# Block scales of an MLP: a max over 128 partitions through DRAM instead of through TensorE, an earlier weight load and seven PSUM banks

## The chip, the cores and the metric

The kernel runs on one core of a Trainium2 chip. The metric is the device time in microseconds (us) of one execution; lower is better. Engines are named as the profile names them: PE is the matrix engine (TensorE), PEld its weight load, DVE is VectorE, ACT is ScalarE, POOL is GpSimd, and SP is the engine that issues the DMAs. PE accumulates in PSUM, which has banks of 128 x 512 float32.

## The reference

One layer of an encoder with 512 tokens and width 1024. The first half (two attention branches, gates and an output projection) is not touched by the change. The second half is

```python
x = x + mixed                       # mixed ends in a product with w_out
h = rms_norm(x, norm_ffn[l])
x = x + jnp.square(jax.nn.relu(h @ w_up[l])) @ w_down[l]   # w_up 1024x4096, w_down 4096x1024
```

## The kernel before

**Products with halves.** The MLP needs more precision than one float16 product gives. Each operand is scaled by a power of two and split into a high and a low float16 half, and each product is three matmuls: high by high, high by low, low by high (`three`, lines 140 to 142). For a block of weights, `split` makes the high half on ACT (line 114) and the low half on DVE (line 115).

**Blocks.** The MLP is a list of 16 blocks (`order`): "u" blocks are 1024 x 512 pieces of w_up, "d" blocks pieces of w_down. In order they are u u u d d u u d d u u u d d d d, numbered 0 to 15. A block has four chunks of 128 x 1024 float32 (512 KB each); PE goes through chunk 0 for four output tiles, then chunk 1, and so on: 16 steps of 6 matmuls, 96 matmuls of 512 columns. Block 0 is done in two halves of 256 columns. Blocks alternate between two sets of SBUF places, so the load of a chunk of block n+2 waits until PE has left the same chunk of block n.

**A block's scale.** `Block.stage(c)` loads a chunk and takes its absolute maximum per partition on DVE (line 818). `Scale.gather` takes the maximum of the four (line 775), lets PE transpose that column into a row (line 777) and takes the row's maximum (line 779). `Scale.spread` lets PE copy the result to all partitions by a product with a column of 2^-14 (line 784), and DVE makes the scale and its inverse (lines 786, 787). Only then can the four `split`s of the block run. There are 20 such scales: one for each block, and one for each quarter q of the hidden activations (`rows[q]`), whose maxima come from ACT's `accum_out` as ACT writes the squared results of the last u block of a quarter (lines 943, 946). The split activations (`split_a`) are the other operand of the d blocks.

**Order.** A scheduler sets each engine's order from the program's order and buffers; instructions under `pin` keep the program's order on their engine. `tick` counts PE's steps; `later(k, f)` runs f at k steps from now, and `prepare` yields once a step. Engines run their instructions strictly in their order. A block's results wait in four PSUM banks (pool `pg`) until ACT or DVE has taken them; three more banks (pool `pm`) serve transposes and scales.

**The transition.** `gemm_rows` (line 199) does the last projection (w_out) in four row tiles. Behind each, x is added (line 856), normalised (`renorm`, line 246), transposed by PE and split. Beside it `staged(blocks[0])` prepares block 0. Block 1's places are still taken by w_out, so it is loaded after `gemm_rows`.

Of the kernel before, what the change touches and what calls it, by code (L numbers as in the profile page):

```python
# [19 lines left out]
P = 128  # L20
# [17 lines left out]
def hybrid_layer(ctx: ExitStack, tc: tile.TileContext, x, norm_mix, w_in, a_q_norm, a_k_norm,  # L38
# [47 lines left out]
    def tick():  # L86
        clock[0] += 1
        due = [w for w in waiting if w[0] <= clock[0]]
        for w in due:
            waiting.remove(w)  # L90
        for w in sorted(due, key=lambda w: w[:2]):
            w[2]()

    def bank(name):
        return pm.tile([P, 512], F32, tag="m", name=name, bufs=3)
# [660 lines left out]

    bound = const.tile([P, 8, 13], F32, name="bound")
    nc.gpsimd.memset(bound, 2.0 ** -60)
    col14 = const.tile([1, P], F32, name="col14")
    nc.gpsimd.memset(col14, 2.0 ** -14)  # L760
    slots = [0]

    class Scale:


        def __init__(self, n):
            self.n = n
            self.m = bound[:, slots[0] % 8, :]
            slots[0] += 1
            self.both = bound[:, (slots[0] - 1) % 8, 9:13]  # L770
            self.by, self.inv = self.both[:, 0:1], self.both[:, 1:2]

        def gather(self):
            top = self.both[:, 2:3]
            nc.vector.tensor_reduce(top, self.m[:, 0:self.n + 1], axis=AX.X, op=ALU.max)
            self.ps = bank("scale")
            pin(nc.tensor.transpose(self.ps[0:1, 0:P], top, ident))
            one = self.both[0:1, 3:4]
            nc.vector.tensor_reduce(one, self.ps[0:1, 0:P], axis=AX.X, op=ALU.max)
            nc.vector.tensor_scalar(one.bitcast(I32), one.bitcast(I32), 0x7F800000, None,  # L780
                                    op0=ALU.bitwise_and)

        def spread(self):
            pin(nc.tensor.matmul(self.ps[:, 256:257], col14, self.both[0:1, 3:4], start=True,  # L784
                                 stop=True))
            nc.vector.tensor_copy(self.inv, self.ps[:, 256:257])
            nc.vector.reciprocal(self.by, self.inv)

    gs = const.tile([P, 4], F32, name="gs")
# [13 lines left out]
    class Block:  # L803
# [4 lines left out]
            self.tags = places[n % 2]  # L808
            self.raw, self.hilo = [], []

        def stage(self, c):
            if c == 0:
                self.scale = Scale(4)
            t = act.tile([P, 4 * 512], F32, tag=self.tags[c], name="w16")
            raw = t[:, 0:1024]
            parts = t[:, 1024:2048].bitcast(F16).rearrange("p (n k c) -> p n k c", n=2, k=KC)
            nc.sync.dma_start(raw.rearrange("p (k c) -> p k c", k=KC), self.src[c])
            nc.vector.tensor_reduce(self.scale.m[:, c:c + 1], raw, axis=AX.X, op=ALU.max,  # L818
                                    apply_absolute_value=True)
            self.raw.append(raw.rearrange("p (k c) -> p k c", k=KC))  # L820
            self.hilo.append((parts[:, 0], parts[:, 1]))

        def split(self, c):
            split(*self.hilo[c], self.raw[c], scale=self.scale.by)

    order = [("u", 0, 0), ("u", 0, 1), ("u", 1, 0), ("d", 0, 0), ("d", 0, 1), ("u", 1, 1),
             ("u", 2, 0), ("d", 1, 0), ("d", 1, 1), ("u", 2, 1), ("u", 3, 0), ("u", 3, 1),
# [2 lines left out]
              Block(w_down_v[:, q * KD:(q + 1) * KD, :], g * 512, n)  # L830
              for n, (kind, q, g) in enumerate(order)]

    def prepare(b):

        b.scale.gather()
        yield
        yield
        b.scale.spread()
        yield
        for c in range(4):  # L840
            b.split(c)
            yield
            yield

    def staged(b):
        for c in range(4):
            b.stage(c)
            yield
            yield
        yield from prepare(b)  # L850

    def add_to_x2(cb, then=None, scale=None):
        def f(i, ps):
# [20 lines left out]
        xn = normed(x2[:, i, :], gbf)  # L874
        later(6, lambda: transposed(xn, i, hh, hl))

    side = staged(blocks[0])
    gemm_rows(chunks, mh, ml, add_to_x2(1, renorm), side=side)
    for _ in side:
        pass  # L880
# [1 line left out]

    raws, rows, parts16 = {}, {}, {}
    for c in range(4):
        blocks[1].stage(c)

    def products(n, tokens_out, ah, al, evac, halves=False, finish=None):
        b = blocks[n]
        pss = [pg.tile([P, 512], F32, tag="g", name="g") for _ in range(4)]
        extra = bank("extra") if finish is not None else None  # L890
        ready = prepare(blocks[n + 1]) if n + 1 < len(blocks) else iter(())
        nxt = blocks[n + 2] if n + 2 < len(blocks) else None
        step = [0]

        def tick16():
            step[0] += 1
            if step[0] >= 4:
                next(ready, None)
            tick()

        if halves:
            for half in range(2):
                cols = slice(half * 256, half * 256 + 256)
                for i in range(4):
                    for c in range(4):
                        part(pss[i][:, cols], False, i, c * KC, KD, b.hilo[c], ah, al, cols)
                        if c % 2:
                            tick16()
                    if half == 1:
                        evac(i, pss[i])  # L910
            if nxt is not None:
                for c in range(4):
                    nxt.stage(c)
        else:
            for c in range(4):
                for i in range(4):
                    if finish is not None and i == 3:
                        for half, ps in enumerate((pss[3], extra)):
                            cs = slice(half * 256, half * 256 + 256)
                            part(ps[:, 0:256], True, i, c * KC, KD,  # L920
                                 [w[:, :, cs] for w in b.hilo[c]], ah, al)
                            if c == 3:
                                finish(ps[:, 0:256], cs)
                        continue
                    part(pss[i], tokens_out, i, c * KC, KD, b.hilo[c], ah, al)
                    if c == 3:
                        evac(i, pss[i])
                    tick16()
                if nxt is not None:
                    nxt.stage(c)  # L930
        for _ in ready:
            pass

    def up(n, q, g):
        if g == 0:
            raws[q] = act.tile([P, KD, S], F32, tag=("mh", "ml")[q % 2], name="a")
            rows[q] = Scale(8)
        inv = sm.tile([P, 1], F32, tag="inv", name="inv")
        nc.vector.tensor_tensor(inv, blocks[n].scale.inv, inv_h, op=ALU.mult)

        def evac(i, ps):
            r = sc.tile([P, 512], F32, tag="sA", name="relu")
            nc.scalar.activation(r, ps, AF.Relu, scale=inv)
            k = 4 * g + i

            nc.scalar.activation(raws[q][:, k, :], r, AF.Square,
                                 accum_out=rows[q].m[:, k:k + 1])
            if k == KD - 1:
                later(4, rows[q].gather)
                later(6, rows[q].spread)  # L950
                for k0 in range(0, KD, KC):
                    later(7 + k0, lambda k0=k0: split_a(q, k0))

        products(n, False, hh, hl, evac, halves=n == 0)

# [56 lines left out]
```

## Time and profile before

| what | value |
|---|---|
| time, median of 3 runs (lowest, highest) | 741.26 us (740.2, 742.75) |
| the profiled execution: its own time, its span | 741.79 us, 740.1 us |
| PE busy | 724.6 us, 98% of the span |
| DVE busy, ACT busy | 429.5 us, 299.8 us |
| block 0 starts; blocks 1 to 15 start; last matmul starts | 382.8; 408.15; 736.37 us |
| granted PE clock | full (2.4 GHz), but half from 419.03 to 422.44 us |

The span is the time from the first to the last instruction; the 1.7 us between it and the execution's own time lie around it. PE's busy time counts overlapping matmuls, so that the time from one matmul's start to the next says more than "busy".

### The profile page before, as it was taken

Reading aid. Unit: us, or ns where it says so; the run is one execution under the profiler, and the core shown is the slowest. Engines: PE = TensorE matmul, PEld = TensorE weight load, DVE = VectorE, ACT = ScalarE, POOL = GpSimd, SP = SyncE. Lnnn points to the kernel's source line nnn. Section 1 sums busy time; section 2 is a strip of 40 time slices with the busy share of each in tenths; the row PEclk is TensorE's granted clock in tenths of the full one; section 3 lists DMA queues with packets and bytes.
Section 4 is the critical chain, followed back from the end, with each engine's and each line's share of the span. In section 5 each row is a group of like instructions: output and inputs, shape, how many; then the busy total and the mean of one; then the engine's idle time right before and its main releaser. Section 6 shows DMA issues by size and latency. Waiting matters only on the chain.

```text
span 740.1 us, 8777 instructions
## 1 busy us (share of the span) xinstructions
PE 724.6 (98%) x3514; PEld 470.6 (64%) x3514; DVE 429.5 (58%) x656; ACT 299.8 (41%) x464; POOL 58.4 (8%) x73
## 2 busy tenths in 40 slices
PE   7999999999999999999999899999999999999998
PEld 4777778888777888888878444444444444444444
DVE  5557475746566545448286637665656658557541
ACT  6444445435455842333054345223650157361020
POOL 4300215000000002103010000000000000000000
PEclk9999999999999999999999999999999999999999
DMA  6703312122211632433030533323233332322211
GB/s 231 242 22 89 111 58 85 58 86 67 76 58 61 201 109 86 134 120 117 0 115 2 160 96 98 101 89 111 86 101 99 101 100 85 107 93 85 86 58 57
DMA packets 37899, 71.03 MB, mean 96 GB/s; under 512 B 3745, under 2 KB 5089, under 8 KB 37858
## 3 DMA queue, kind: packets, MB, share of 16 engines
q1 hardware_dynamic: 37858, 70.47, 30.5%
q8 instruction: 27, 0.44, 0.2%
q14 instruction: 14, 0.11, 0.0%
HBM read 68.36 MB, written 2.10 MB: 95 GB/s over the span
## 4 chain that ended last, share of the span: by engine, by line
PE 83%; DMA 7%; DVE 6%; ACT 1%; POOL 1%; issue 1%; SPq 0%; DVEq 0%; POOLq 0%
PE g L140 25%; PE g L142 25%; PE g L141 24%; DMA w<-in_w_down_dram 4%; DVE bound L818 2%; DMA w<-in_w_up_dram 2%; PE poa L663 2%; DVE w L115 1%; DMA wst<-in_w_in_dram 1%; DVE xn L246 1%; PE scale L784 1%; PE ps L591 1%; PE ps L587 1%; PE ptp L75 1%; PE pa L499 1%
## 5 line engine op out<-in xcount | busy, mean ns | idle before, releaser
L114 ACT ACTIVATE w<-w,bound 128x1024 f16<-128x1024 f32 x64 | 68.5, 1138 | 141.6 <-PE scale L784 49.8
L818 DVE TENSOR_REDUCE bound<-w 128x1 f32<-128x1024 f32 x64 | 77.7, 1217 | 68.4 <-DMA w<-in_w_down_dram 35.9
L142 PE MATMUL g<-h,w 128*128 128x512 f16 (+1 forms) x288 | 102.9, 358 | 0.7 <-DVE w L115 0.7
L141 PE MATMUL g<-h,w 128*128 128x512 f16 (+1 forms) x288 | 102.7, 357 | 0.3 <-DVE h L112 0.3
L140 PE MATMUL g<-h,w 128*128 128x512 f16 (+1 forms) x288 | 102.6, 358 | 0.0
L140 PE MATMUL g<-w,a 128*128 128x512 f16 (+1 forms) x256 | 96.2, 376 | 0.7 <-DVE x L858 0.7
L142 PE MATMUL g<-w,a 128*128 128x512 f16 (+1 forms) x256 | 96.2, 376 | 0.0
L141 PE MATMUL g<-w,a 128*128 128x512 f16 (+1 forms) x256 | 96.2, 376 | 0.0
L112 DVE TENSOR_TENSOR wl<-wst,wh 128x1024 fp32r<-128x1024 f32 x48 | 59.6, 1244 | 59.5 <-ACT wh L111 59.3
L115 DVE SCALAR_TENSOR_TENSOR w<-w,bound 128x1024 f16<-128x1024 f32 x64 | 78.8, 1279 | 2.7 <-ACT w L114 2.6
L111 ACT CAST wh<-wst 128x1024 fp32r<-128x1024 f32 x48 | 50.3, 1050 | 70.2 <-PE g L141 47.2
L140 PE MATMUL g<-uh,wh 128*128 128x512 f32 x160 | 64.9, 406 | 0.0
L142 PE MATMUL g<-uh,wl 128*128 128x512 f32 x160 | 62.6, 391 | 0.0
L141 PE MATMUL g<-ul,wh 128*128 128x512 f32 x160 | 62.5, 391 | 0.0
L140 PE MATMUL g<-wh,uh 128*128 128x512 f32 x128 | 52.9, 413 | 0.3 <-DVE qt L458 0.3
L141 PE MATMUL g<-wl,uh 128*128 128x512 f32 x128 | 50.1, 392 | 0.0
L142 PE MATMUL g<-wh,ul 128*128 128x512 f32 x128 | 50.0, 392 | 0.0
L142 PEld LDWEIGHTS <-w 128*128 128x128 f16 x288 | 28.3, 98 | 29.2 <-issue 1.4
L140 PEld LDWEIGHTS <-w 128*128 128x128 f16 x288 | 28.3, 98 | 25.8 <-issue 0.8
L142 PEld LDWEIGHTS <-a 128*128 128x128 f16 x264 | 25.8, 98 | 29.5
L141 PEld LDWEIGHTS <-w 128*128 128x128 f16 x288 | 28.3, 98 | 25.3 <-issue 0.8
L141 PEld LDWEIGHTS <-a 128*128 128x128 f16 x264 | 25.8, 98 | 28.7 <-issue 1.0
(239 smaller groups left out, 1128.0 us busy)
## 6 DMA issues: line engine op xcount, KB each, us to landing
wst<-in_w_in_dram SPq DMA_DIRECT2D x41, 512.0 KB, 3.7
w<-in_w_up_dram SPq DMA_DIRECT2D x32, 512.0 KB, 3.7
w<-in_w_down_dram SPq DMA_DIRECT2D x32, 512.0 KB, 3.8
wst<-in_w_branch_dram SPq DMA_DIRECT2D x8, 512.0 KB, 3.8
wst<-in_w_out_dram SPq DMA_DIRECT2D x8, 512.0 KB, 4.0
xs<-in_x_dram SPq DMA_DIRECT2D x4, 512.0 KB, 7.0
x<-in_x_dram SPq DMA_DIRECT2D x4, 512.0 KB, 7.2
out_dram<-x SPq DMA_DIRECT2D x7, 256.0 KB, 2.0
```

Source lines behind the costliest of these rows:

```text
L75: ins = nc.tensor.transpose(out[:, i, :], block, ident)
L111: first(nc.scalar.copy(hi, src))
L112: first((engine or nc.vector).tensor_tensor(lo, src, value(hi), op=ALU.subtract))
L114: nc.scalar.activation(hi, src, AF.Identity, scale=scale)
L115: nc.vector.scalar_tensor_tensor(lo, src, scale, value(hi), op0=ALU.mult, op1=ALU.subtract)
L140: nc.tensor.matmul(ps, ah, bh, start=start, stop=False)
L141: nc.tensor.matmul(ps, ah, bl, start=False, stop=False)
L142: nc.tensor.matmul(ps, al, bh, start=False, stop=stop)
L246: first(nc.vector.scalar_tensor_tensor(xn[j], src[:, cs], r, g, op0=ALU.mult, op1=ALU.mult))
L499: nc.tensor.matmul(pa[:, hs, :], kd[:, c, t * P:(t + 1) * P], qz[:, c, t], start=True, stop=True)
L663: nc.tensor.matmul(po[:, h, :], pT[0][:, k, :], av[:, k, h * P:(h + 1) * P], start=(k == 0), stop=(k == t))
L818: nc.vector.tensor_reduce(self.scale.m[:, c:c + 1], raw, axis=AX.X, op=ALU.max, apply_absolute_value=True)
```

## The change

Four parts. (1) `Scale.gather` no longer uses PE: the column of maxima is written to DRAM by a DMA from POOL's queue and read back by a second one as a row on every partition; `spread` takes the maximum of that 128 x 128 tile on DVE. (2) Loads and maxima are separate (`load`, `top`); the maximum of a chunk is put 3 steps behind its load. In `prepare` the gather comes at step 6 instead of 4, the spread at step 12 instead of 6, and the four splits at steps 12, 13, 14 and 15 instead of 7, 9, 11 and 13. For `rows` the gather comes 2 steps after the last result instead of 4 and the spread 8 instead of 6. (3) Block 1 is loaded during `gemm_rows`, into a place of its own (`ul`). (4) Results rotate through seven banks: four of `pg`, three of `pm`.

```diff
         def gather(self):
             top = self.both[:, 2:3]
-            nc.vector.tensor_reduce(top, self.m[:, 0:self.n + 1], axis=AX.X, op=ALU.max)
-            self.ps = bank("scale")
-            pin(nc.tensor.transpose(self.ps[0:1, 0:P], top, ident))
-            one = self.both[0:1, 3:4]
-            nc.vector.tensor_reduce(one, self.ps[0:1, 0:P], axis=AX.X, op=ALU.max)
+            pin(nc.vector.tensor_reduce(top, self.m[:, 0:self.n + 1], axis=AX.X, op=ALU.max))
+            there = tc.dram_tile([1, P], F32, name="tops")
+            nc.gpsimd.dma_start(there.rearrange("o p -> p o"), top)
+            self.row = wp.tile([P, P], F32, tag="st", name="row", bufs=4)
+            nc.gpsimd.dma_start(self.row, there.broadcast_to([P, P]))
+
+        def spread(self):
+            one = self.both[:, 3:4]
+            pin(nc.vector.tensor_reduce(one, self.row, axis=AX.X, op=ALU.max))
             nc.vector.tensor_scalar(one.bitcast(I32), one.bitcast(I32), 0x7F800000, None,
                                     op0=ALU.bitwise_and)
-
-        def spread(self):
-            pin(nc.tensor.matmul(self.ps[:, 256:257], col14, self.both[0:1, 3:4], start=True,
-                                 stop=True))
-            nc.vector.tensor_copy(self.inv, self.ps[:, 256:257])
+            nc.vector.tensor_scalar(self.inv, one, 2.0 ** -14, None, op0=ALU.mult)
             nc.vector.reciprocal(self.by, self.inv)
...
+        def top(self, c):
+            pin(nc.vector.tensor_reduce(self.scale.m[:, c:c + 1], self.raw[c], axis=AX.X,
+                                        op=ALU.max, apply_absolute_value=True))
...
-    def prepare(b):
-
+    def prepare(b, wait):
+
+        for _ in range(wait):
+            yield
         b.scale.gather()
-        yield
-        yield
+        for _ in range(6):
+            yield
         b.scale.spread()
-        yield
         for c in range(4):
             b.split(c)
             yield
+
+    def first_blocks():
+        for c in range(4):
+            blocks[0].load(c)
+        raw = act.tile([P, 4, 1024], F32, tag="ul", name="raw1")
+        for c in range(4):
+            blocks[1].load(c, raw[:, c, :])
+        yield
+        yield
+        for c in range(4):
             yield
...
+            blocks[0].top(c)
+        yield from prepare(blocks[0], 1)
...
-    side = staged(blocks[0])
+    side = first_blocks()
...
     for c in range(4):
-        blocks[1].stage(c)
+        blocks[1].place(c)
+        blocks[1].top(c)
+    turn = [0]
+
+    def psum():
+        turn[0] += 1
+        if turn[0] % 7 < 4:
+            return pg.tile([P, 512], F32, tag="g", name="g")
+        return bank("g")
...
-        pss = [pg.tile([P, 512], F32, tag="g", name="g") for _ in range(4)]
...
-        ready = prepare(blocks[n + 1]) if n + 1 < len(blocks) else iter(())
+        pss = [psum() for _ in range(4)]
...
+        ready = prepare(blocks[n + 1], 5) if n + 1 < len(blocks) else iter(())
...
+        def load_next(c):
+            if nxt is not None:
+                nxt.load(c)
+                later(3, lambda: nxt.top(c))
...
-                later(4, rows[q].gather)
-                later(6, rows[q].spread)
+                later(2, rows[q].gather)
+                later(8, rows[q].spread)
                 for k0 in range(0, KD, KC):
-                    later(7 + k0, lambda k0=k0: split_a(q, k0))
+                    later(8 + k0, lambda k0=k0: split_a(q, k0))
```

**ACT at the end of block 5**, a u block that ends a quarter. The four `w` tiles are the high halves of block 6; relu (line 943 before, 964 after) and square (946, 967) take block 5's results; `a` tiles are the activations' high halves, done in block 6. Before:

```order
L114 ACTIVATE w_3813<-w_3813,bound 128x1024
L114 ACTIVATE w_3845<-w_3845,bound 128x1024
L114 ACTIVATE w_3876<-w_3876,bound 128x1024
L114 ACTIVATE w_3909<-w_3909,bound 128x1024
L943 ACTIVATE relu<-g,inv 128x512
L946 ACTIVATE a,bound<-relu 128x512
```

and in the changed kernel:

```order
L114 ACTIVATE w_3815<-w_3815,bound 128x1024
L114 ACTIVATE w_3847<-w_3847,bound 128x1024
L964 ACTIVATE relu<-g,inv 128x512
L114 ACTIVATE w_3880<-w_3880,bound 128x1024
L967 ACTIVATE a,bound<-relu 128x512
L964 ACTIVATE relu<-g,inv 128x512 x2
L967 ACTIVATE a,bound<-relu 128x512 x2
L114 ACTIVATE w_3917<-w_3917,bound 128x1024
L964 ACTIVATE relu<-g,inv 128x512
L967 ACTIVATE a,bound<-relu 128x512
L114 ACTIVATE a_4128<-a,bound 128x1024 x4
```

The high halves of the next block now stand between the results; the last square, which completes the maxima of `rows`, stands behind all four.

**DVE in block 6**, behind the low halves of block 6. `bound` holds the maxima and scales, `w_3979` and up (before) or `w_4015` and up (after) are chunks of blocks 7 and 8, `a` the activations' low halves, and `w_3947` or `w_3950` is chunk 0 of block 7. Before:

```order
L786 COPY bound<-scale 128x1
L787 RECIPROCAL bound<-bound 128x1
L786 COPY bound<-scale 128x1
L115 SCALAR_TENSOR_TENSOR a_4116<-a,bound,a_4116 128x1024
L818 TENSOR_REDUCE bound<-w_4095 128x1
L787 RECIPROCAL bound<-bound 128x1
L115 SCALAR_TENSOR_TENSOR a_4116<-a,bound,a_4116 128x1024 x2
L115 SCALAR_TENSOR_TENSOR w_3947<-w_3947,bound 128x1024
```

and in the changed kernel, from the spread of `rows` on (line 781 reads the row that came back from DRAM; the second one is block 7's):

```order
L781 TENSOR_REDUCE bound<-row 128x1
L782 TENSOR_SCALAR bound<-bound 128x1
L784 TENSOR_SCALAR bound<-bound 128x1
L785 RECIPROCAL bound<-bound 128x1
L115 SCALAR_TENSOR_TENSOR a_4128<-a,bound,a_4128 128x1024
L826 TENSOR_REDUCE bound<-w_4099 128x1
L115 SCALAR_TENSOR_TENSOR a_4128<-a,bound,a_4128 128x1024
L826 TENSOR_REDUCE bound<-w_4138 128x1
L115 SCALAR_TENSOR_TENSOR a_4128<-a,bound,a_4128 128x1024
L781 TENSOR_REDUCE bound<-row 128x1
L115 SCALAR_TENSOR_TENSOR a_4128<-a,bound,a_4128 128x1024
L782 TENSOR_SCALAR bound<-bound 128x1
```

Behind the last of these rows come two more small instructions, line 985, and then the low half of `w_3950`. Block 7's scale, which before stood among the first of the activations' low halves, now stands behind all four of them and two maxima.

**POOL in blocks 5, 6 and 7.** Before, POOL has no instruction there. Now it has these; `tops_4076` is the column of `rows`, `tops_4114` that of block 7:

```order
L775 DMA tops_3965<-bound_2715 128x1
L777 DMA row_3967<-tops_3965 128x128
L775 DMA tops_4076<-bound_2715 128x1
L775 DMA tops_4114<-bound_2715 128x1
L777 DMA row_4078<-tops_4076 128x128
L777 DMA row_4116<-tops_4114 128x128
```

Where a quarter's scale and a block's scale fall into one block (blocks 2, 6, 10 and 12), the reading back of the first stands behind the writing of the second.

## Rows read from the trace of the kernel before

**Rows 1.** Page: span, and busy time of each engine, share, instructions.

```profile
span 740.1 us, 8777 instructions
...
PE 724.6 (98%) x3514; PEld 470.6 (64%) x3514; DVE 429.5 (58%) x656; ACT 299.8 (41%) x464; POOL 58.4 (8%) x73
```

**Rows 2.** Stretches: length, busy us of each engine, granted clock, DMA share, GB/s.

```profile
408.15:736.50 328.35, 324.08 (x1520) 147.72 (x1517) 191.37 (x264) 114.88 (x159) 0.00 (x0) 0.99 0.30 94
...
419.03:422.44 3.41, 3.41 (x10) 1.17 (x9) 3.38 (x5) 3.37 (x4) 0.00 (x0) 0.50 0.00 0
```

**Rows 3.** Timeline of PE, end of block 0 and end: start, duration, instruction.

```profile
408.04 0.27 PE L142 MATMUL g<-h,w 128*128 128x256 f16 x1
408.15 0.38 PE L140 MATMUL g<-h,w 128*128 128x512 f16 x1
408.37 0.38 PE L141 MATMUL g<-h,w 128*128 128x512 f16 x1
...
736.37 0.27 PE L142 MATMUL extra<-w,a 128*128 128x256 f16 x1
```

**Rows 4.** Timeline of PE in block 1, around the scale of block 2.

```profile
415.06 0.38 PE L142 MATMUL g<-h,w 128*128 128x512 f16 x1
417.42 0.27 PE L777 MATMUL scale<-ident,bound 128*1 128x128 f32 x1 [1.98 <-DVE bound L775]
...
420.28 0.63 PE L142 MATMUL g<-h,w 128*128 128x512 f16 x1
420.70 0.63 PE L140 MATMUL g<-h,w 128*128 128x512 f16 x1
```

**Rows 5.** Timeline of PE, start of block 13.

```profile
673.07 0.38 PE L142 MATMUL g<-w,a 128*128 128x512 f16 x1
674.16 0.38 PE L140 MATMUL g<-w,a 128*128 128x512 f16 x1 [0.71 <-DVE x L858]
```

**Rows 6.** Groups by line, blocks 1 to 15: busy us, mean ns, idle before.

```profile
L115 DVE SCALAR_TENSOR_TENSOR w<-w,bound 128x1024 f16<-128x1024 f32 x56 | 68.8, 1279 | 1.6 <-ACT w L114 1.5
L818 DVE TENSOR_REDUCE bound<-w 128x1 f32<-128x1024 f32 x56 | 68.2, 1218 | 66.1 <-DMA w<-in_w_down_dram 35.9 <-DMA w<-in_w_up_dram 29.7
...
L858 DVE SCALAR_TENSOR_TENSOR x<-g,inv,x 128x512 f32<-128x512 f32 x31 | 22.6, 747 | 29.9 <-PE g L142 29.9
...
L784 PE MATMUL scale<-bound,col 1*128 1x1 f32 x36 | 6.8, 256 | 0.0
...
L777 PE MATMUL scale<-ident,bound 128*1 128x128 f32 x18 | 4.9, 271 | 3.6 <-DVE bound L775 3.1
```

**Rows 7.** Timelines of DVE and PE in the transition.

```profile
367.07 1.42 DVE L246 SCALAR_TENSOR_TENSOR xn<-x,rx,gb_ffn 128x512 f32<-128x512 f32 x2 [2.14 <-POOL rx L101]
369.69 0.69 DVE L856 TENSOR_TENSOR x<-x,g 128x512 f32<-128x512 f32 x1 [1.20 <-PE g L142]
...
388.45 3.47 DVE L818 TENSOR_REDUCE bound<-w 128x1 f32<-128x1024 f32 x3
...
382.82 0.28 PE L140 MATMUL g<-h,w 128*128 128x256 f16 x1
```

**Rows 8.** DMA from issue to landing: chunk loads (line 817), small columns (327), small rows (354).

```profile
DMA to landing us min/median/max: 3.5/3.8/7.3
...
DMA to landing us min/median/max: 2.0/2.3/3.9
...
DMA to landing us min/median/max: 2.9/3.3/3.9
```

**Rows 9.** Timeline of ACT at the start of block 6, and the load that starts with it.

```profile
519.71 3.88 DMA w<-in_w_down_dram
...
520.54 0.63 ACT L946 ACTIVATE a<-relu 128x512 f32<-128x512 f32 x1
521.08 0.19 ACT L946 ACTIVATION_READ_ACCUMULATOR a<-relu 128x1 f32 x1
527.44 4.26 ACT L114 ACTIVATE a<-a,bound 128x1024 f16<-128x1024 f32 x4 [6.18 <-DVE bound L787]
531.62 4.25 ACT L114 ACTIVATE w<-w,bound 128x1024 f16<-128x1024 f32 x4
```

More of the change, by code (lines that the diff above doesn't have):

```diff
@@ L758, in hybrid_layer @@
     nc.gpsimd.memset(bound, 2.0 ** -60)
-    col14 = const.tile([1, P], F32, name="col14")
-    nc.gpsimd.memset(col14, 2.0 ** -14)
     slots = [0]
@@ L767, in __init__ @@
             self.n = n
-            self.m = bound[:, slots[0] % 8, :]
+            slot = slots[0] % 8
             slots[0] += 1
-            self.both = bound[:, (slots[0] - 1) % 8, 9:13]
+            self.m, self.both = bound[:, slot, 0:9], bound[:, slot, 9:13]
             self.by, self.inv = self.both[:, 0:1], self.both[:, 1:2]
@@ L809, in __init__, with load, place @@
             self.raw, self.hilo = [], []
-        def stage(self, c):
+        def load(self, c, raw=None):
             if c == 0:
                 self.scale = Scale(4)
+            if raw is None:
+                t = self.place(c)
+                raw = t[:, 0:1024]
+            nc.sync.dma_start(raw.rearrange("p (k c) -> p k c", k=KC), self.src[c])
+            self.raw.append(raw)
+        def place(self, c):
             t = act.tile([P, 4 * 512], F32, tag=self.tags[c], name="w16")
-            raw = t[:, 0:1024]
             parts = t[:, 1024:2048].bitcast(F16).rearrange("p (n k c) -> p n k c", n=2, k=KC)
[L817 to L820, printed above, removed]
             self.hilo.append((parts[:, 0], parts[:, 1]))
+            return t
+        def top(self, c):
+            pin(nc.vector.tensor_reduce(self.scale.m[:, c:c + 1], self.raw[c], axis=AX.X,
+                                        op=ALU.max, apply_absolute_value=True))
         def split(self, c):
-            split(*self.hilo[c], self.raw[c], scale=self.scale.by)
+            split(*self.hilo[c], self.raw[c].rearrange("p (k c) -> p k c", k=KC),
+                  scale=self.scale.by)
     order = [("u", 0, 0), ("u", 0, 1), ("u", 1, 0), ("d", 0, 0), ("d", 0, 1), ("u", 1, 1),
@@ L842, in prepare @@
             yield
-            yield
[L845 to L850, printed above, removed]
+    def first_blocks():
[7 more added lines that the diff above has]
+        for c in range(4):
+            yield
+            blocks[0].top(c)
+        yield from prepare(blocks[0], 1)
     def add_to_x2(cb, then=None, scale=None):
@@ L884, in hybrid_layer @@
     for c in range(4):
-        blocks[1].stage(c)
+        blocks[1].place(c)
[6 more added lines that the diff above has]
+        return bank("g")
     def products(n, tokens_out, ah, al, evac, halves=False, finish=None):
         b = blocks[n]
-        pss = [pg.tile([P, 512], F32, tag="g", name="g") for _ in range(4)]
-        extra = bank("extra") if finish is not None else None
-        ready = prepare(blocks[n + 1]) if n + 1 < len(blocks) else iter(())
+        pss = [psum() for _ in range(4)]
+        extra = psum() if finish is not None else None
+        ready = prepare(blocks[n + 1], 5) if n + 1 < len(blocks) else iter(())
         nxt = blocks[n + 2] if n + 2 < len(blocks) else None
-        step = [0]
         def tick16():
-            step[0] += 1
-            if step[0] >= 4:
-                next(ready, None)
+            next(ready, None)
             tick()
+        def load_next(c):
+            if nxt is not None:
+                nxt.load(c)
+                later(3, lambda: nxt.top(c))
         if halves:
@@ L910, in products @@
                         evac(i, pss[i])
-            if nxt is not None:
-                for c in range(4):
-                    nxt.stage(c)
+            for c in range(4):
+                load_next(c)
         else:
@@ L928, in products @@
                     tick16()
-                if nxt is not None:
-                    nxt.stage(c)
+                load_next(c)
         for _ in ready:
```

## The prediction

> **What bounds the kernel.** The page's busy times come first: PE is busy for 98% of the span, DVE for 58% [rows 1]. But overlapping matmuls hide small waits in "busy", so the timeline is read from start to start. A matmul of 512 columns starts 0.2155 us after the one before it, one of 256 columns 0.11 us [rows 3]. Blocks 1 to 15 are 15 x 96 = 1440 matmuls, 310.3 us at that pace; they take 328.35 us [rows 2, 3]. So 18.0 us are lost there, and this is all that the change can win behind block 0. It has three parts. The one long wait for a scale is 417.42 - 415.06 - 0.22 = 2.1 us [rows 4]. After it PE's granted clock is 0.50 (1.2 instead of 2.4 GHz) for 3.41 us [rows 2]; matmuls start 0.42 us apart [rows 4], so half of 3.41, 1.7 us, is lost. The start of block 13 waits for a bank, 1.09 - 0.22 = 0.9 us [rows 5]. What is left, 18.0 - 2.1 - 1.7 - 0.9 = 13.3 us, lies around 18 transposes and 36 copies, with only 3.6 us of it shown as idle [rows 6]: some 0.7 us for a scale, by the matmuls themselves and by PE filling and emptying around them.
>
> **What is removed.** No scale is on PE any more, and no result lacks a bank. I count 17.5 of the 18.0 us as gone; 0.5 us stays for short irregularities. The load of block 2 still starts late, as block 0 holds its places to the end, but PE no longer waits for its maximum in the middle of block 1.
>
> **The transition.** Here DVE's queue decides. The maxima of block 0's chunks 1 to 3 now stand behind the first normalisation, which ends at 368.5, and ahead of the second add, which ran at 369.69 [rows 7]. Three maxima take 3.47 us [rows 7], so the add ends at 372.55 and the gather at 372.7. The way over DRAM has until 381.5, since the spread stands behind the third normalisation; that is 8.8 us, enough. With the spread (0.3), the other two small operations, a transposed tile's low halves (1.3) and an add in between, the scale exists near 383.6 and ACT's first high half at 384.8. PE, without the two scale matmuls, is free at 382.45 instead of 382.82 [rows 7], so it waits 2.4 us. Block 0's low halves follow 1.2 us apart with a normalisation (1.4) before the last, while PE wants one each 1.1 us: 1.5 us more. Four maxima of block 1's chunks (4.6) then stand ahead of the third transposed tile: 1.1 us more. The sum is 382.45 + 192 x 0.109 + 16 transposes of 0.11 + 5.0 = 410.2, against 408.15 [rows 3]: **2.1 us lost**. Block 1's own scale is then covered: its gather ends at 397.5, and its first half is wanted at 410.
>
> **Ordinary blocks.** From a block's start, u = 0: the last chunk of the next block lands at 4.0 (3.8 for a load [rows 8]), its maximum ends at 5.2, the gather at 5.4. DVE's queue then has the maximum of a chunk that PE frees at 10.4 and that lands at 14.15; so the spread runs at 15.3 whatever DRAM takes, up to 10 us. ACT's first high half is there at 17.4 and DVE's low half at 18.7, wanted at 20.7. The way over DRAM costs nothing here; what covers it is that load, with 2 us to spare.
>
> **Blocks 2, 6, 10 and 12** also carry a quarter's scale, and here I find new waits. Before, the last results were through ACT at 521.27, 1.6 us into block 6, and all high halves at 535.9, 16 us in [rows 9]; blocks 7 and so on never waited. Now ACT starts at u = 16.3 of block 5 with four high halves (1.05 each) and four results (0.67 + 0.63 + 0.19 less overlap, 1.33 each [rows 9]) mixed, 9.7 us; the last maximum is there 5.4 us into block 6. DVE has a low half and a maximum before the gather, which ends at 6.6. Two transfers follow, each waiting for the one before: X = 6.6 + 0.2 + 2 legs. Behind X in DVE's queue stand: the spread and three small ones (0.75), ACT's first high half of the activations (1.15), four low halves (1.2 each, 1.28 alone [rows 6]), two maxima (1.15 each), the block's own spread (0.3) and its small ones (0.5): X + 9.85. Then ACT makes block 7's first high half (1.25): X + 11.1; the low half comes 1.3 later. PE wants the first at 20.7 and the second 0.2 later. So PE waits X - 9.55 and then 1.1: **X - 8.45** in all. Block 11 is a u block and uses the high half twice before the low one: X - 8.65. In block 12 two results of 0.65 each [rows 6] stand between the small operations: X - 7.2. The four sum to 4X - 32.75.
>
> **The price of a leg.** No trace of before has a DMA from POOL's queue. The nearest are SP's small columns, 2.0 to 3.9 us with a median of 2.3, and small rows, 2.9 to 3.9 [rows 8]; a chunk load is in flight during either leg here. Nothing lands under 2.0, so the low end is X = 10.8 and waits of 10.4 us; at 3.9, X = 14.6 and 25.6 us. I take 2.5, nearer to the columns since the DMA engines are only 30% busy [rows 2]: X = 11.8, waits of **14.4 us**. The Trainium skill ("DMA: Bandwidth & Descriptors", section "Anatomy of one DMA — SWDGE (gpsimd) path") gives a DMA from GpSimd's queue a fixed cost of about 2.0 us. By that estimate the waits would be the 10.4 us of the low end; no run here shows it.
>
> **The clock.** The one fall of the clock came after 2.1 us of waiting [rows 4]. Each new wait is 2.3 us (3.5 at block 13) plus 1.1, so I expect it after all four: 4 x 1.7 = **6.8 us**. The low bound is none, as the wait of 0.9 us at block 13 cost none [rows 5]; the high one two falls more, with the transition's wait of 2.4, 3.4 us.
>
> **The sum**, from the profiled execution's own 741.8: - 17.5 + 2.1 + 14.4 + 6.8 = 747.6. That execution was 0.5 above the median, so **747 us**, 0.8% slower. About 0.3%, 2.2 us, is what a measurement can tell from no change here (739.0 to 743.5).
>
> **Rivals.** A: the four waits exist, but the clock falls after none or one of them, or the legs take near 2.0. With 2.0 and no fall: 741.8 - 17.5 + 2.1 + 10.4 = 736.8, less 0.5. For it speaks that the two pieces of each wait are split by a matmul; against it that each first piece is longer than the wait that preceded the fall of before. It decides for "faster" at a leg of 2.3 without falls, or 1.5 with four. B: the waits don't come, because the scheduler's order lets the quarter's chain start earlier than I walked it: 741.8 - 17.5 + 2.1 = 726. Against it speaks that both queues run strictly in the printed order and that X must be under 8.45, a leg of 0.8, which no row shows. C: a leg takes 3.9 or more, because DVE's work holds up POOL's: 741.8 - 17.5 + 2.1 + 25.6 + 6.8 = 758.8. For it: POOL must issue both columns before it reads back the first, and DVE is busy throughout; against it: the median of the columns. The Trainium skill ("SBUF — State Buffer", section "SBUF: two separate sides") warns that GpSimd cannot write its DMAs' descriptors while DVE runs an operation that holds their shared ports. By it C would be the case; no run here shows it.
>
> **How the numbers follow.** The forecast (legs of 2.3 to 3.3, the clock falling after most waits) has 0.50 and by itself gives 742 to 755; A 0.30 (735 to 743), B 0.10 (724 to 732), C 0.10 (754 and up). Leaving out B and most of C gives 733 to 757. Faster: B and two thirds of A, 0.30; same: the rest of A and the forecast's lower edge, 0.17; slower: 0.53.
>
> **What would show it.** In the profile after: PE waits for ACT's or DVE's `w` at the first matmuls of blocks 3, 7, 11 and 13, 2 to 4 us each, and nowhere else behind block 1; 18 scale matmuls gone and blocks without a quarter at 20.7 us; stretches at half clock behind these waits; DVE's idle time before line 781 in blocks 2, 6, 10 and 12 alone. I would be wrong if a leg took under 2 us or over 4, if ordinary blocks also waited (a way over DRAM above 10 us), if the clock stayed at full, or if block 0 ended before 409 or after 412.

## The result and the profile after

The changed kernel takes **833.69 us** (median of 4, 829.91 to 839.37) against 740.73 us before: ratio 1.126, 95% interval 1.119 to 1.133. Forecast were 747 us, range 733 to 757. "Slower" was right; the loss is 93 us instead of 6. In the times below one run, 766.16 us of the kernel with the unread column, is left out as it was in a slower state.

The page of the profile after: its span and busy times (cf. [rows 1]), and the chain that ended last, by engine; the last row is that chain in the kernel before:

```profile
span 831.8 us, 8754 instructions
...
PE 736.4 (89%) x3454; PEld 469.7 (56%) x3454; DVE 428.0 (51%) x656; ACT 296.9 (36%) x464; POOL 79.9 (10%) x112
...
PE 48%; issue 19%; DMA 17%; DVE 8%; ACT 5%; POOL 1%; SPq 0%; POOLq 0%; ACTq 0%; DVEq 0%
...
PE 83%; DMA 7%; DVE 6%; ACT 1%; POOL 1%; issue 1%; SPq 0%; DVEq 0%; POOLq 0%
```

DVE and ACT have no more work than before, and POOL has 21.5 us more, its DMAs. PE is busy for 89% instead of 98% of the span. The DMAs have 17% of the chain instead of 7%. The view of waits says who waits for them (total us, times, longest):

```profile
POOL row L777 <- DMA tops<-bound: 120.2, 20, 9.0
...
DVE bound L781 <- DMA row<-tops: 89.4, 11, 14.7
PE g L140 <- ACT w L114: 77.1, 14, 14.4
...
DVE bound L826 <- DMA w<-in_w_up_dram: 53.8, 10, 11.5
```

POOL waits 6 us per scale for the column to be in DRAM, DVE for the row, and at the end PE for high halves, 14 times. The last line is a second thing: DVE also waits for weight chunks, as it did before, but for up to 11.5 us instead of 7.9. The lines of the three DMAs, column (775), row (777) and chunks (816; cf. [rows 8]), each with its time from issue to landing:

```profile
L775 POOL DMA_DIRECT2D tops<-bound x20: 542/543/749, 372.7 to 789.1; - x20
...
DMA to landing us min/median/max: 6.7/7.8/9.3
...
L777 POOL DMA_DIRECT2D row<-tops x20: 534/537/613, 380.4 to 797.1; - x20
...
DMA to landing us min/median/max: 3.8/5.1/6.6
...
DMA to landing us min/median/max: 3.5/4.6/12.0
```

The way over DRAM takes 7.8 + 0.3 + 5.1 = 13 us where the prediction had 5. The write of 512 bytes is its slowest part, slower than a chunk of 512 KB. Timelines of POOL, DVE and PE show what that does to an ordinary block (the scale of block 5, made in block 4):

```profile
511.00 0.54 POOL L775 DMA_DIRECT2D tops<-bound  x1 [17.26 <-DVE bound L773]
519.32 0.53 POOL L777 DMA_DIRECT2D row<-tops  x1 [7.78 <-DMA tops<-bound]
...
522.83 1.22 DVE L826 TENSOR_REDUCE bound<-w 128x1 f32<-128x1024 f32 x1 [10.61 <-DMA w<-in_w_up_dram]
525.06 0.29 DVE L781 TENSOR_REDUCE bound<-row 128x1 f32<-128x128 f32 x1 [1.02 <-DMA row<-tops]
...
522.38 0.38 PE L142 MATMUL g<-w,a 128*128 128x512 f16 x1
527.21 0.61 PE L140 MATMUL g<-h,w 128*128 128x512 f16 x1 [4.45 <-ACT w L114]
```

The chunk that was issued 1.4 us behind the column, at 512.43, lands at 522.8 and holds up DVE's queue; the row lands 2.2 us later still. PE stands for 4.5 us and runs at half clock afterwards (matmuls 0.4 us apart). Stretches of all blocks 1 to 15, of 6 us behind two columns, of 6 us behind one (that of the timeline above), and of 2.5 us with a chunk alone (columns as in [rows 2]):

```profile
414.09:828.00 413.91, 334.56 (x1464) 146.09 (x1464) 195.04 (x268) 119.13 (x171) 19.46 (x36) 0.90 0.35 77
...
564.50:570.50 6.00, 6.00 (x29) 2.72 (x28) 0.00 (x0) 0.00 (x0) 0.07 (x1) 1.00 0.91 16
...
513.00:519.00 6.00, 6.00 (x30) 2.69 (x28) 0.00 (x0) 0.00 (x0) 0.00 (x0) 1.00 0.65 63
508.00:510.50 2.50, 2.50 (x13) 1.09 (x12) 2.50 (x3) 0.00 (x0) 0.00 (x0) 1.00 0.68 209
```

Behind two columns the DMA engines are shown as busy for 91% of the time and move 16 GB/s, behind one for 65% and 63 GB/s; a chunk alone makes them 68% busy at 209 GB/s. None of the 18 chunk loads that were issued while a column was under way landed before that column.

From start to start, blocks 1 to 15 now take 413.9 us: 310.3 at full pace, 84.8 in 25 waits of over 0.8 us (52.0 of it at blocks 3, 7, 11 and 13, 32.8 at the others), 17.4 in 85 matmuls at half clock, and 1.4 of irregularities. Block 1 starts at 414.09 (before: 408.15 [rows 3]).

### The profile page after: what moved, and what is told of

Same layout as the page of the kernel before. It is cut to its first block, busy times and chain, and to the rows that moved or that the text cites. A ratio compares the mean times of both kernels' runs of the same rounds, so it can differ in the third digit from the quotient of the medians.

```text
span 831.8 us, 8754 instructions
## 1 busy us (share of the span) xinstructions
PE 736.4 (89%) x3454; PEld 469.7 (56%) x3454; DVE 428.0 (51%) x656; ACT 296.9 (36%) x464; POOL 79.9 (10%) x112
## 4 chain that ended last, share of the span: by engine, by line
PE 48%; issue 19%; DMA 17%; DVE 8%; ACT 5%; POOL 1%; SPq 0%; POOLq 0%; ACTq 0%; DVEq 0%
PE g L142 14%; PE g L140 14%; PE g L141 14%; DMA tops<-bound 10%; DMA row<-tops 4%; ACT w L114 2%; DVE bound L826 2%; DVE w L115 2%; PE poa L663 1%; DVE a L115 1%; DMA w<-in_w_down_dram 1%; DMA w<-in_w_up_dram 1%; ACT relu L964 1%; ACT a L967 1%; DMA wst<-in_w_in_dram 1%
## 5 line engine op out<-in xcount | busy, mean ns | idle before, releaser
L114 ACT ACTIVATE w<-w,bound 128x1024 f16<-128x1024 f32 x60 | 65.5, 1138 | 213.8 <-DVE bound L785 88.4
L140 PE MATMUL g<-w,a 128*128 128x512 f16 (+1 forms) x264 | 101.7, 389 | 45.1 <-ACT w L114 45.1
L140 PE MATMUL g<-h,w 128*128 128x512 f16 (+1 forms) x288 | 107.2, 374 | 32.7 <-ACT w L114 32.0
L826 DVE TENSOR_REDUCE bound<-w 128x1 f32<-128x1024 f32 x60 | 72.3, 1213 | 89.3 <-DMA w<-in_w_up_dram 53.8
L142 PE MATMUL g<-h,w 128*128 128x512 f16 (+1 forms) x288 | 105.9, 369 | 3.6 <-DVE w L115 3.6
L141 PE MATMUL g<-h,w 128*128 128x512 f16 (+1 forms) x288 | 106.8, 372 | 0.0
L141 PE MATMUL g<-w,a 128*128 128x512 f16 (+1 forms) x264 | 101.5, 384 | 5.1 <-DVE w L115 5.1
L142 PE MATMUL g<-w,a 128*128 128x512 f16 (+1 forms) x264 | 101.6, 385 | 0.0
L115 DVE SCALAR_TENSOR_TENSOR w<-w,bound 128x1024 f16<-128x1024 f32 x60 | 75.5, 1280 | 29.2 <-ACT w L114 29.2
L140 PEld LDWEIGHTS <-w 128*128 128x128 f16 x288 | 29.1, 101 | 63.1 <-ACT w L114 35.5
L781 DVE TENSOR_REDUCE bound<-row 128x1 f32<-128x128 f32 x20 | 5.6, 282 | 89.5 <-DMA row<-tops 89.4
L142 PEld LDWEIGHTS <-w 128*128 128x128 f16 x288 | 29.0, 101 | 37.9 <-DVE w L115 9.3
```

Of the source, the lines that this page charges most:

```text
L114: nc.scalar.activation(hi, src, AF.Identity, scale=scale)
L115: nc.vector.scalar_tensor_tensor(lo, src, scale, value(hi), op0=ALU.mult, op1=ALU.subtract)
L140: nc.tensor.matmul(ps, ah, bh, start=start, stop=False)
L141: nc.tensor.matmul(ps, ah, bl, start=False, stop=False)
L142: nc.tensor.matmul(ps, al, bh, start=False, stop=stop)
L781: pin(nc.vector.tensor_reduce(one, self.row, axis=AX.X, op=ALU.max))
```

## The experiments

**What makes the write slow: not the queue.** The theory was that the 128 pieces of 4 B are slow; the rival, that POOL's queue is.

```diff
-            nc.gpsimd.dma_start(there.rearrange("o p -> p o"), top)
+            nc.sync.dma_start(there.rearrange("o p -> p o"), top)
```

> Edit: the column of maxima is written to DRAM from SP's queue instead of POOL's; the read of the row stays on POOL's. Theory (the write of 128 pieces of 4 B is slow whatever queue it comes from): issue to landing stays at 6.7 to 9.3 us, PE waits before the same blocks, and the time stays at 820 to 845 us. Rival (POOL's queue is slow, because DVE's work or the queue itself holds it up): the column lands in 2.0 to 3.9 us, as SP's small columns did in the kernel before, the way over DRAM falls to about 8 us, ordinary blocks wait no more and the time falls to 755 to 790 us.

Measured: 853.28 us (one run; before 740.92), and the column is no faster from SP:

```profile
L775 SPq DMA_DIRECT2D tops<-bound x20: 338/339/419, 372.6 to 810.4; - x20
...
DMA to landing us min/median/max: 7.5/8.7/18.6
```

The queue is not it. That the time rose beyond the range was not foreseen; the column's landing now reaches 18.6 us. Nor is it other traffic or DVE: the last column of the changed kernel has both out of its way. Its timelines, and the DMA view of the 7 us behind its issue (the digits are 40 slices, the last row all packets of that stretch):

```profile
788.63 0.16 DVE L773 TENSOR_REDUCE bound<-bound 128x1 f32<-128x5 f32 x1
801.28 0.29 DVE L781 TENSOR_REDUCE bound<-row 128x1 f32<-128x128 f32 x1 [12.49 <-DMA row<-tops]
...
789.08 0.54 POOL L775 DMA_DIRECT2D tops<-bound  x1 [17.32 <-DVE bound L773]
797.07 0.54 POOL L777 DMA_DIRECT2D row<-tops  x1 [7.45 <-DMA tops<-bound]
...
DMA  0000100000000000000000000000000000000000
...
DMA packets 32, 0.00 MB, mean 0 GB/s; under 512 B 32, under 2 KB 32, under 8 KB 32
```

DVE does nothing from 788.8 to 801.3, no chunk moves, the packets that the view shows come about 1 us behind the issue, and the write still takes 7.7 us.

**Four rows instead of 128 pieces.** DVE turns the column in blocks of 32 by 32 first.

```diff
+            four = sm.tile([P, 32], F32, tag="four", name="four")
+            nc.vector.transpose(four, top.broadcast_to([P, 32]))
-            nc.gpsimd.dma_start(there.rearrange("o p -> p o"), top)
+            nc.gpsimd.dma_start(there.rearrange("o (g c) -> (o g) c", g=4), four[0:P:32, :])
```

> Edit: DVE first turns the column in blocks of 32 by 32, so that four rows of 128 B go to DRAM instead of 128 pieces of 4 B; queue, places and the read are kept. Theory (small pieces): the write lands in 2 to 3 us, the way over DRAM takes 7 to 9 us instead of 12 to 15, the chunk loads beside it fall from up to 12 us to under 6, ordinary blocks wait no more, and blocks 3, 7, 11 and 13 still do: X = 6.6 + 0.5 + 2.3 + 0.3 + 5.1 = 14.8, 4X - 32.75 = 26 us, with 6.8 for the clock 741.8 - 17.5 + 2.1 + 26 + 6.8 = 759, range 750 to 775 us. Rival (POOL's queue): the write still lands after 7 us or more and the time stays at 820 to 845 us.

Measured: 750.11 us, ratio 1.0125 [1.0107, 1.0143]. This change of shape alone gives back 84 of the 93 us. The expectation had 759, mostly because it kept the row at 5.1 us. The same three lines (column 777, row 779), and PE at the start of block 7:

```profile
L777 POOL DMA_DIRECT2D tops<-four x20: 573/578/778, 372.8 to 711.1; - x20
...
DMA to landing us min/median/max: 1.6/1.9/3.8
...
L779 POOL DMA_DIRECT2D row<-tops x20: 553/555/634, 374.9 to 713.0; - x20
...
DMA to landing us min/median/max: 3.2/3.5/5.0
...
539.89 0.38 PE L142 MATMUL g<-h,w 128*128 128x512 f16 x1
543.65 0.59 PE L140 MATMUL g<-w,a 128*128 128x512 f16 x2 [3.38 <-ACT w L114]
544.97 0.59 PE L141 MATMUL g<-w,a 128*128 128x512 f16 x1 [0.73 <-DVE w L115]
```

The row, whose DMA is unchanged, falls from 5.1 to 3.5 us. Why is not shown: many rows of the changed kernel came with held-up chunk loads beside them, but the last one, with no chunk moving, still took 4.2 us. PE now waits at blocks 3, 7, 11 and 13 alone, 17.0 us in all.

**Which pieces are slow.** Five kernels add to the kernel before a write beside each gather that nobody reads, so only its side effect can cost time. They differ in the pieces:

```diff
+            nc.gpsimd.dma_start(there.rearrange("o p -> p o"), top)               # 128 x 4 B in 512 B
+            nc.gpsimd.dma_start(there, wide)          # wide [P, 128]: 128 x 512 B; [P, 16]: 128 x 64 B
+            nc.gpsimd.dma_start(there.rearrange("o p -> p o"), top[0:P:32, :])    # 4 x 4 B
+            nc.gpsimd.dma_start(there[:, 0:1], top)   # there [P, 16]: 128 x 4 B, 64 B apart
```

> Edit: the kernel before, which makes its scales on PE, and beside each gather the same column is written to DRAM, which nobody reads or waits for. It prices the column's side effect by itself. Theory (while its pieces are written, other transfers stand still): the column lands in 6.7 to 9.3 us, chunk loads that are issued up to 7 us behind it take 8 to 12 us instead of 3.8, and as DVE's maxima of these chunks stand ahead of low halves the time rises by 2 to 15 us, to 743 to 756. Rival (only the waiter pays): chunk loads stay at 3.5 to 7.3 us and the time stays within 739 to 743.5.

> Edit: the kernel before with a write to DRAM beside each gather that nobody reads, as in the run with the extra column, but with 128 pieces of 512 B (the column copied along 128 places by DVE first) instead of 128 pieces of 4 B. Theory (the size of a piece matters, not their number): it lands in 2 to 4 us, chunk loads stay at 3.5 to 7.3 us and the time stays at 739 to 744 us. Rival (128 pieces are slow whatever their size, or POOL's queue is): 7 us or more to landing, and 750 us or more as with the extra column.

> Edit: the kernel before with an unread write beside each gather of 128 pieces of 64 B, between the extra column (4 B: 7.5 to 16.4 us to landing) and the wide one (512 B: 1.8 to 4.6). Theory (what costs is a piece under 512 B, whatever it holds): 6 us or more. Rival (cost falls with the size, 4 B alone is bad): under 4 us.

> Edit: the kernel before with an unread write beside each gather of 4 pieces of 4 B, from partitions 0, 32, 64 and 96, instead of 128 pieces of 4 B. Theory (each small piece costs by itself, and 128 of them queue up): it lands in 1.5 to 3 us, and chunk loads stay under 7.5 us. Rival (one write of 4 B is as slow as many): 6 us or more.

> Edit: the kernel before with the unread column of 128 pieces of 4 B beside each gather again, but each piece goes to a place of its own, 64 B from the next, instead of all 128 into one stretch of 512 B in DRAM. Theory (neighbours in one stretch have to be written one after another): it lands in 1.6 to 4 us as the pieces of 64 B did, and chunk loads stay under 8 us. Rival (a piece of 4 B is slow wherever it goes, and 128 of them queue up): 7 us or more, and chunk loads of 10 us or more, as with the extra column.

| unread write | lands, us min/median/max | chunk loads | time, us | ratio |
|---|---|---|---|---|
| none (before) | | 3.5/3.8/7.3 | 738.6 to 743.5 (single runs) | |
| 128 x 4 B in one stretch of 512 B | 7.5/9.0/16.4 | 3.5/4.6/16.4 | 756.25 | 1.0211 [1.0174, 1.0249] |
| 128 x 512 B | 1.8/3.5/4.6 | 3.6/3.8/6.3 | 740.88 | 1.0002 [0.9984, 1.0019] |
| 128 x 64 B | 1.7/3.3/5.2 | 3.4/3.8/6.6 | 738.72 (one run) | |
| 4 x 4 B in 16 B | 1.6/3.6/4.2 | 3.5/3.8/7.8 | 741.72 (one run) | |
| 128 x 4 B, 64 B apart | 1.7/3.6/4.6 | 3.5/3.8/7.2 | 740.60 (one run) | |

The last row decides: the same 128 pieces of 4 B, each to a place of its own, cost nothing. My theory at the start, "a small piece is slow", and the one held for the 64 B pieces, "under 512 B is slow", both fall. So does the one held for the four pieces, that each small piece costs by itself; they land a little later than it expected. Slow are many pieces that go into one short stretch of DRAM; four rows of 128 B in such a stretch, above, were not. The side effect alone, with nobody waiting for the column, is 15 us, the upper end of what was expected: the chain of the first of these kernels runs at one place through a chunk load of 16.4 us.

```profile
610.63 16.40 DMA w<-in_w_down_dram
627.03 0.02 issue
627.06 1.22 DVE bound L820
```

**The rest of the change.** First the scales went back to PE with all else kept; then each of two other parts was put alone into the kernel before.

```diff
 # scales back on PE: gather and spread as in the kernel before, from the new places and with seven banks
+            self.ps = bank("scale")
+            pin(nc.tensor.transpose(self.ps[0:1, 0:P], top, ident))
 # seven banks alone, in the kernel before
-        pss = [pg.tile([P, 512], F32, tag="g", name="g") for _ in range(4)]
+        pss = [psum() for _ in range(4)]
 # early load and separate maxima alone (cut; this line is against the changed kernel): scales on PE,
 # results in the four banks, and the old places
-        ready = prepare(blocks[n + 1], 5) if n + 1 < len(blocks) else iter(())
+        ready = prepare(blocks[n + 1], 3) if n + 1 < len(blocks) else iter(())
```

> Edit: the changed kernel with its scales made on PE again, by the two matmuls of the kernel before; separate loads and maxima, places in the program (gather at step 6, spread at step 12), the early load of block 1 and the seven banks are kept. Theory (the whole loss is the way over DRAM): waits of over 2 us behind block 0 are gone; 741.8 less 2.1, 1.7 and 0.9 for the waits of before, plus about 2 for the transition gives 739, range 731 to 743 us. Rival (the later places in the program cost by themselves: halves that stand at steps 12 to 15 come late): PE still waits 2 us or more before most blocks and the time is over 755 us.

> Edit: only the separate loads and maxima and the early load of block 1 are kept of the change; the scales are on PE at the places of the kernel before (gather at step 4, spread at step 6, splits at 7, 9, 11 and 13, rows 4, 6 and 7) and the results in four banks. Theory (this part is nearly neutral, the loss is the way over DRAM alone): 737 to 743 us. Rival (the early load or the moved maxima cost by themselves, for instance in the transition): 746 us or more, with waits in the transition that the kernel before has not.

> Edit: the kernel before with only the seven banks. Scales stay on PE and take their bank from the same three as part of the results do. Theory for this part alone: the wait for a bank at the start of block 13 (0.9 us) goes, but a scale that has to take a bank of a result which PE or ACT still holds is made late, as in the run with the scales back on PE: PE waits 3 us or more before some blocks and the time is 755 to 785 us. Rival (that run's waits came from the late places in the program, not from the banks): 738 to 743 us.

Scales back on PE: 780.82 us, ratio 1.0535 [1.0512, 1.0558]; the time is on the side of the rival, but the edit itself made a new wait, so that it does not decide. The scale's transpose has to take one of the three banks that results now hold too. Timelines of ACT, PE and DVE around the second scale of block 2:

```profile
455.32 0.67 ACT L966 ACTIVATE relu<-g,inv 128x512 f32<-128x512 f32 x1
...
456.04 0.08 PEld L777 LDWEIGHTS scale<-ident,bound 128*1 128x1 f32 x1 [0.48 <-ACT relu L966]
456.04 0.27 PE L777 MATMUL scale<-ident,bound 128*1 128x128 f32 x1
...
456.35 0.28 DVE L779 TENSOR_REDUCE bound<-scale 1x1 f32<-1x128 f32 x1 [14.65 <-PE scale L777]
```

The column was ready at 441.7; PE makes the transpose only when ACT has read a result out of its bank, 14 us later. Seven banks alone, with scales on PE: 756.03 us, 1.0201 [1.0169, 1.0233], as expected. Early load and separate maxima alone: 740.55 us, 0.9998 [0.9983, 1.0012], nothing. So neither of these parts wins here by itself, and seven banks are only safe where no scale needs one. How the 40 us of the first kernel split between banks and later places was not settled. In the run with four rows, which keeps the later places and the banks, blocks that carry no quarter's scale and follow none take 20.7 us from start to start, their pace without waits; so the later places cost those blocks nothing there.

**Without DRAM and without PE.** The maximum over the partitions is made by DVE, and the places move too (code cut at the dots):

```diff
+            pin(nc.vector.transpose(sq[:, 0:32], top.broadcast_to([P, 32])))
+            nc.vector.tensor_reduce(sq[:, 32:33], sq[:, 0:32], axis=AX.X, op=ALU.max)
+            nc.vector.tensor_copy(sq[0:64, 33:34], sq[64:128, 32:33])
+            nc.vector.tensor_copy(sq[64:128, 33:34], sq[0:64, 32:33])
+            nc.vector.tensor_reduce(sq[:, 34:35], sq[:, 32:34], axis=AX.X, op=ALU.max)
+            for g in range(4):
+                to, of = 32 * g, 32 * (g ^ 1)
+                nc.vector.tensor_copy(sq[to:to + 32, 35:36], sq[of:of + 32, 34:35])
+            nc.vector.tensor_reduce(one, sq[:, 34:36], axis=AX.X, op=ALU.max)
...
         b.scale.gather()
-        for _ in range(6):
-            yield
+        yield
         b.scale.spread()
...
-                later(8, rows[q].spread)
+                later(3, rows[q].spread)
                 for k0 in range(0, KD, KC):
-                    later(8 + k0, lambda k0=k0: split_a(q, k0))
+                    later(4 + k0, lambda k0=k0: split_a(q, k0))
```

> Edit: the changed kernel, but the maximum over the partitions is made on DVE alone: a turn of the column in blocks of 32 by 32, a maximum per row, and six small copies between groups of 32 partitions with two more maxima; some 14 small operations that wait for each other, about 2.5 us for a scale. No PE, no DMA. The spread follows one step behind the gather, and the splits of rows begin 4 steps behind the last result. Theory (without the way over DRAM the rest of the change is worth what the prediction counted): no waits of over 2 us behind block 0 and no fall of the clock there, 741.8 - 17.5 + 2.1 = 726, range 721 to 732 us. Rival (moving the scales off PE wins little, since the 0.7 us per scale were not PE's): 736 us or more without long waits.

Measured: 728.24 us, ratio 0.983 [0.981, 0.985]. Blocks 1 to 15, as a stretch, and PE's start of block 0:

```profile
412.26:723.10 310.84, 310.84 (x1466) 143.17 (x1463) 214.45 (x426) 114.98 (x159) 0.00 (x0) 1.00 0.32 100
...
384.51 0.49 PE L140 MATMUL g<-h,w 128*128 128x256 f16 x3 [2.40 <-ACT h L111]
387.24 0.37 PE L141 MATMUL g<-h,w 128*128 128x256 f16 x1 [2.25 <-DVE h L112]
```

PE loses 0.5 us in 15 blocks, at full clock. What is left lies in the transition, and it is the transposed tile `h` that comes late there, not block 0's weights as the next expectation has it. In the last kernel block 0's spread follows its gather at once:

```diff
-        yield from prepare(blocks[0], 1)
+        blocks[0].scale.gather()
+        blocks[0].scale.spread()
+        for c in range(4):
+            yield
+            blocks[0].split(c)
```

> Edit: the version with the maximum on DVE alone, and block 0's spread follows its gather at once, ahead of the second normalisation, instead of a step later. In the version before it PE waited 2.6 us for block 0's first high half and 2.4 for its first low half, and ran 6.8 us at half clock behind that. Theory (the spread's place among the normalisations makes those waits): scale and low halves are there before PE is free at 382, both waits go and with them the half clock, 728.2 - 2.6 - 2.4 - 3.4 = 720, range 718 to 724 us. Rival (the four low halves now stand ahead of the third normalisation, which makes the third and fourth token tile late): new waits inside block 0 or before its second half, 726 to 731 us.

Measured: **726.00 us**, ratio 0.9795 [0.9775, 0.9815], the fastest here, 2 us above the range. The first wait shrinks to 0.4 us, the second stays. PE, DVE, ACT and POOL in its transition:

```profile
382.64 0.49 PE L140 MATMUL g<-h,w 128*128 128x256 f16 x3 [0.38 <-ACT h L111]
385.65 0.27 PE L141 MATMUL g<-h,w 128*128 128x256 f16 x1 [2.52 <-DVE h L112]
...
377.99 4.87 DVE L115 SCALAR_TENSOR_TENSOR w<-w,bound 128x1024 f16<-128x1024 f32 x4
383.59 1.42 DVE L246 SCALAR_TENSOR_TENSOR xn<-x,rx,gb_ffn 128x512 f32<-128x512 f32 x2 [0.72 <-POOL rx L101]
384.92 1.28 DVE L112 TENSOR_TENSOR h<-pt,h 128x512 f16<-128x512 f32 x2
...
376.81 4.27 ACT L114 ACTIVATE w<-w,bound 128x1024 f16<-128x1024 f32 x4 [2.29 <-issue]
380.99 1.04 ACT L240 ACTIVATE sq<-x 128x1024 bf16<-128x1024 f32 x1
...
382.21 0.71 POOL L100 TENSOR_SCALAR rx<-ss 128x1 f32<-128x1 f32 x1 [7.72 <-ACT sq L240]
```

The time lies at the lower end of the rival's range, and as it says the third normalisation comes late, with the low half of `h` behind it. But the queue that ends last is not the one it named. DVE's four low halves are done at 382.9; DVE then stands for 0.7 us, until POOL has made the normalisation's factor `rx`. POOL waited for the sum of squares (`sq`), and that stood behind block 0's four high halves on ACT.

## Why the prediction failed

**The step that failed is the price of a leg.** It took 2.5 us, between 2.0 and 3.9, from small columns and rows on SP's queue [rows 8]. Those rows were reads out of DRAM into SBUF; none was a write of many pieces into one short stretch of DRAM. The columns of [rows 8] even consist of pieces of 4 B that adjoin in DRAM, but they are read, not written. The column took 7.8 us and the row behind it 5.1. The high end did not bound it: "the nearest rows" were near in size and far in kind. The Trainium skill ("DMA: Bandwidth & Descriptors", section "Anatomy of one DMA — SWDGE (gpsimd) path") gives about 2.0 us for a DMA from this queue. The write of four rows, 1.6 to 3.8 with a median of 1.9, agrees with that; the column, 6.7 at the least, does not, and the measurement decides.

**What hangs on it.** Ordinary blocks were to be covered for a way of up to 10 us; the way is 13, so they wait too (4.5 us at block 5). One late scale also delays the next: in block 4 the gather ends 9.9 us in (510.7 - 500.8) instead of 5.4, as block 4's own low halves, made late, stand ahead of the maxima in DVE's queue. The cover itself was mis-seen as well: it was a chunk load of 3.8 us, and the column makes that load 10.4. The prediction let a transfer hide behind another without asking what it does to it, and the run with the unread column puts that at 15 us by itself. Three of the signs of being wrong that it named are there: a leg over 4 us, waits at ordinary blocks, and block 0 ending behind 412 us.

**What held.** The walk through the queues. Lines of DVE, first in the changed kernel, then with four rows:

```profile
577.08 0.28 DVE L781 TENSOR_REDUCE bound<-row 128x1 f32<-128x128 f32 x1 [14.68 <-DMA row<-tops]
...
532.57 0.29 DVE L783 TENSOR_REDUCE bound<-row 128x1 f32<-128x128 f32 x1 [4.92 <-DMA row<-tops]
```

For blocks 6 and 7 the row of the quarter lands 25.1 us into block 6 in the changed kernel (577.08 - 551.95), so X - 8.45 gives 16.7, of which 0.9 is spent by a wait inside block 6; PE waits 15.3. With four rows the row is there at 532.57, 13.2 us into block 6 (532.57 - 519.39); the formula says 4.7, and PE waits 4.4 (3.5 and 0.9). That run is nearly the predicted one, its legs 1.9 + 3.5 against 2 x 2.5: waits at blocks 3, 7, 11 and 13 alone, 17.0 us against 14.4; the clock falls after all four; 750 against 747 us. That block 1 starts at 409.97 there, against 410.2, is partly luck: PE waits 3.5 us in that transition instead of 5.0, but runs 3.4 us at half clock, which was not in the central forecast. The 17.5 us counted as removed are there when nothing waits: 310.84 us for blocks 1 to 15 on DVE alone, where the prediction left 310.3 + 0.5.

**The transition.** 2.1 us were forecast; the changed kernel loses 5.9. The spread of block 0 has its row at 384.2 instead of 381.5, because the way took 11.5 us there and not 8.8 at most. POOL stood behind the column until 380.4, and as it also makes the factor of each normalisation, the third one ran at 381.97 (with four rows: 379.97).

**The clock.** Forecast were four falls, 6.8 us. Eight half-clock stretches lie in blocks 1 to 15, 82 us long, and a ninth of 3.4 us in block 0; but PE is busy for only 41 of the 82 us, and its matmuls lose 17.4 us.

**The rivals.** C (a leg of 3.9 or more, 754 us and up) is the one that holds the measured time, but not for its reason, that DVE's work holds up POOL, and its sum gave 758.8. The Trainium skill ("SBUF — State Buffer", section "SBUF: two separate sides") spoke for it; the last column, written in 7.7 us while DVE was idle, and the slow column from SP's queue speak against that as the cause here. A and B needed short legs and were never near.

## What to carry to other kernels

Take the price of a DMA from a row of the same direction, piece size and spacing in DRAM; where there is none, the high end is open. Ask of every transfer that is to be hidden what it does to the transfers that hide it. A column over 128 partitions goes to DRAM as four rows (after a 32 by 32 turn) or with its pieces 64 B apart (how those read back was not tried), not as 512 adjoining bytes; and where a scale is all that is wanted, some 14 small DVE operations made it without either, and with the early load and the seven banks kept that kernel is 2% faster than the one before (the maximum on DVE alone in the kernel before was not tried).

## What was not expected of the hardware

A write of 512 bytes took longer (7.8 us) than a load of 512 KB (3.8), held back the chunk loads behind it (behind two columns packets moved at 16 instead of 209 GB/s while the DMA engines showed 91% busy), and did so only where its 4 B pieces adjoin: 64 B apart they landed in 3.6 us, 1.7 at the least. The Trainium skill ("DMA: Bandwidth & Descriptors", section "Specifications") says that transfers under 512 B are done as read-modify-write. Pieces that share a stretch would then have to follow one another; that would fit, but no run here shows the mechanism, and pieces of 64 B, which that rule covers too, cost nothing extra.
